# A hybrid encoder layer on one core: the merge of the next block's inverses is emitted directly behind a block's chain

## The chip, the core and the metric

The kernel runs on one of the eight cores of a Trainium2 chip. A core has TensorE (PE, matrix multiply; its weight loads are listed as PEld), VectorE (DVE), ScalarE (ACT), GpSimd (POOL) and SyncE (SP), which only issues transfers here. Each engine executes its own instructions in a fixed order and waits for others by semaphores. Transfers between memory and the core's buffers run on 16 DMA engines. TensorE writes to a small accumulator memory (PSUM), from which VectorE or ScalarE take the results.

The metric is the time of one execution in device microseconds; less is better.

## The reference

One layer of an encoder in float32 for 1024 positions of width 1024: a half-step gated feed-forward, a mixer with two groups of eight heads, and a second half-step feed-forward, each with norms around it. One group is dilated attention, the other a forward and a backward scan of the generalized delta rule. The scan is where the change lies:

```python
def _rwkv7_step(state, inp):
    r, w, k, v, kk, kka = inp
    sa = jnp.einsum('dbhvk,dbhk->dbhv', state, kk)
    state = state * w[..., None, :] - sa[..., :, None] * kka[..., None, :] + v[..., :, None] * k[..., None, :]
    y = jnp.einsum('dbhvk,dbhk->dbhv', state, r)
    return state, y
...
x = x + post1(FFN1(pre1(x))) * 0.5
x = x + post2(concat(attn, rwkv) @ w_out)
x = x + post3(FFN2(pre3(x))) * 0.5
```

(The last three lines are the layer in short form.) A state is 64 by 64 for each head and direction.

## The kernel before

**Stages.** The first feed-forward, the input projection and the attention come first, then the scan (from about 1250 to 1560 us of the span), then the finish of the scan's heads, the output projection, and the second feed-forward. Only the scan's order is touched.

**Chunks and blocks.** The scan goes by chunks of 64 positions, two chunks to a block: 16 chunks, 8 blocks (`NB`), both directions and all eight heads at once. Within a chunk the recurrence is solved as a triangular system, for which an inverse of a 64 by 64 unit triangular matrix is needed for each chunk, direction and head: 32 of them a block. Each block passes four steps:

- `prep(n)` (L789) loads the block's inputs, forms the decayed factors on VectorE and ScalarE, multiplies them on TensorE into `lp` (L836), masks the products on VectorE into `lm` (L838), transposes keys into `bt` (L844, L846), and stores the diagonal 32 by 32 parts of `lm` to memory (`x_d`, L852, on SyncE's queue).
- `solve(n)` (L856) loads these parts spread over partitions (`X`, L861), inverts the 32 by 32 triangles in 31 steps of two VectorE instructions each (L872, L874) and transposes the result back into `X` (L876).
- `merge(n)` (L879) makes the 64 by 64 inverses of the 32 by 32 ones. Per block: 128 small matmuls into the accumulator `pa` (L889), a ScalarE copy of it into `tt` (L890); 64 matmuls with the off-diagonal part of `lm` (L894), two copies into `tt` (L896) and one into `am` (L897); 64 matmuls (L900) and two copies with the sign changed into `tt` (L902). Each group of matmuls waits for the copy ahead of it.
- `chain(n)` (L918) runs the recurrence for the block's two chunks. ScalarE first overwrites a part of `lm` with `pr` (L928), which has to wait until the merge has read `lm`. Then for each chunk: `xu` from the state `sv` (L941), a copy `xs` (L944), the product of the inverses `tt` with `xs` (L952), a signed copy into `uv` (L954), the new state `st` and the output `y` (L937 at the helper's line), the state scaled on VectorE (L968), and `y` copied into `yb` (L970) and stored.

**Buffers.** Block data (`lm`, `pr`, `bt`, `gc`) has three places, `R0`, `R1` and `B0`, taken in turn, so `prep(n + 3)` can start writing only when `chain(n)` has let its place go. `X` has two buffers: `solve(n + 3)` takes over that of `solve(n + 1)`, which `merge(n + 1)` reads last. `tt` has two tiles, by the parity of the block. The accumulator `pa` has one buffer, so the first matmuls of a merge wait until the merge before has copied it out.

**Attended tiles.** `project_attended` (L1066) multiplies a tile of 128 rows of the attention's output by its half of the output weights: a load (`yat`), a scaling, four transposes (`yq`), a split into two parts, and twice twelve matmuls (`po`, shown at L1064). It does not depend on the scan and is spread over the loop: tiles 0 and 1 after chain 0, then 2, 3 and 4, then 5 and 6 after chain 4, and 7 after chain 5.

**What sets the order.** The program names the engine of each instruction, and its order of emission gives each a rank. When the program is built, a planner goes through the whole graph on a timeline of its own. For each engine it takes, among the instructions whose inputs and buffers are ready on that timeline, the one emitted earliest. So instructions of several steps lie mixed on an engine, and a step emitted earlier goes first where both could run. On the chip that order is fixed: an instruction whose input comes later than planned holds up everything behind it on its engine.

The loop (L1289 to L1306) first merges block 0, prepares and solves block 2 (0 and 1 came before), then goes over the blocks: merge of the block (from block 1), its chain, then `upto(n + 3)`, which prepares and solves block n + 3 if there is one, then the attended tiles. For n of 5 and more `upto` does nothing.

Of the kernel before, what the change touches and what calls it, by code (L numbers as in the profile page):

```python
# [163 lines left out]
class _Kernel:  # L164
# [1002 lines left out]
    def run(self):  # L1167
# [5 lines left out]
        with self.top as top:  # L1173
# [86 lines left out]
            NB, s_sr, s_pr, s_zr, s_pm = NC_ // BLK, ExitStack(), ExitStack(), ExitStack(), ExitStack()  # L1260
# [5 lines left out]
            pm = self.pool(s_pm, "ps_m", 1, space=PSUM, **R)  # L1266
# [4 lines left out]
            blk = {}  # L1271
# [7 lines left out]
            sc = self.pool(s_sc, "scan")  # L1279
# [9 lines left out]
            def upto(m):  # L1289
                while nxt[0] <= min(m, NB - 1):  # L1290
                    n = nxt[0]
                    blk[n] = self.prep(n, sp, pp, (R0, R1, B0)[n % 3])
                    blk[n]["inv"] = self.solve(n, sp)
                    nxt[0] += 1
# [3 lines left out]
            upto(2)  # L1298
            WA = self.out_weights(eo, 0, self.aog)
            for n in range(NB):  # L1300
                if n:
                    self.merge(n, blk[n], sc, pm)
                self.chain(n, blk.pop(n), sc, pc)
                upto(n + 3)
                for t in {0: [0, 1], 1: [2], 2: [3], 3: [4], 4: [5, 6], 5: [7]}.get(n, []):
                    self.project_attended(eo, sc, pe, t, WA, rs_a)  # L1306
# [133 lines left out]
```

## Time and profile before

| | |
|---|---|
| median of 3 runs | 2345.42 us (2341.84 to 2350.2) |
| profiled execution | 2343.05 us, of which the span from first to last instruction is 2341.3 us |
| mean granted TensorE clock | 0.969 |
| 62 instructions of one solve (L872, L874), each | about 0.25 us |
| a chain, from L941 of its first chunk to its last scaled state | about 14 to 20 us |
| a block, from chain to chain, blocks 1 to 5 | 36 to 45 us |

How to read the profile: times are microseconds, durations in group listings are nanoseconds. "L889" is line 889 of the kernel. `out<-in` names the tiles written and read. In a timeline, a row is start, duration, engine, line, operation, tiles, shape and count; the bracket at the end is the time that the engine stood idle just before, and what ended it. "issue" is time in which the engine waited for nothing that the profile names. In a table of waits a row is: engine and what waited, what it waited for, the sum in us, how often, the longest. The granted clock (PEclk) is TensorE's, as a share of full speed. Ends of matmuls are modelled, since they overlap.

### The profile page before, as it was taken

What the parts mean: (1) busy time and instruction counts of PE and PEld (TensorE: products, weight loads), DVE (VectorE), ACT (ScalarE), POOL (GpSimd) and SP (SyncE); (2) the same over time, 40 slices, a digit from 0 to 9 for tenths busy, and PEclk for the clock granted to TensorE, in tenths of its full rate; (3) what the DMA queues carried; (4) which work ended last, traced back from release to release, by engine and by line L of the source; (5) the groups of instructions that cost most, each with busy time, mean ns of one, the idle gap of its engine ahead of it and who ended that gap; (6) DMA issues with size and microseconds to landing.
All of it is one profiled execution on the core that took longest, in us unless ns stands there. A gap on an engine that the chain in (4) does not pass through costs nothing. (4 is left out here: it accounts for less than half of the span.)

```text
span 2341.3 us, 41376 instructions
## 1 busy us (share of the span) xinstructions
PE 2206.1 (94%) x15556; PEld 1783.6 (76%) x15556; DVE 1768.5 (76%) x2870; ACT 1031.8 (44%) x1958; POOL 551.5 (24%) x662
## 2 busy tenths in 40 slices
PE   6999999999999998999996998988799999999997
PEld 4788888878877676788775777765578888887886
DVE  8899999965676244666668877737899999996565
ACT  4323232354577412666555555454442323235443
POOL 6244444410000010111111111122424444441000
PEclk8999999999999999999997999989899999999999
DMA  5244545486672514443268655467435454548665
GB/s 154 97 165 167 171 148 172 153 269 191 195 229 83 219 46 123 119 115 99 62 174 222 174 155 161 113 205 267 154 113 170 168 171 147 173 154 269 193 191 178
DMA packets 357148, 381.97 MB, mean 163 GB/s; under 512 B 73042, under 2 KB 264402, under 8 KB 356948
## 3 DMA queue, kind: packets, MB, share of 16 engines
q1 hardware_dynamic: 309088, 278.53, 39.5%
q0 software_dynamic: 27504, 88.14, 9.9%
q10 hardware_dynamic: 20356, 12.66, 1.8%
q8 instruction: 122, 2.00, 0.4%
q14 instruction: 78, 0.64, 0.1%
HBM read 256.49 MB, written 122.75 MB: 162 GB/s over the span
## 5 line engine op out<-in xcount | busy, mean ns | idle before, releaser
L186 ACT ACTIVATE wh<-raw 128x512 fp32r<-128x512 f32 (+1 forms) x273 | 168.2, 627 | 271.2 <-DVE raw L62 93.6
L187 DVE TENSOR_TENSOR wl<-raw,wh 128x512 fp32r<-128x512 f32 (+1 forms) x273 | 278.7, 1023 | 6.0 <-ACT wh L186 5.2
L81 PE MATMUL gu<-xh,wh 128*128 128x512 f32 x704 | 278.3, 396 | 1.2 <-ACT xh L186 0.8
L81 PE MATMUL gu<-xl,wh 128*128 128x512 f32 x704 | 276.6, 393 | 0.0
L81 PE MATMUL gu<-xh,wl 128*128 128x512 f32 x704 | 276.2, 392 | 0.0
L415 PE MATMUL pd<-gl,gwh 128*128 128x512 f32 x616 | 240.3, 390 | 2.3 <-DVE gl L187 2.3
L415 PE MATMUL pd<-gh,gwh 128*128 128x512 f32 x616 | 239.5, 390 | 0.6 <-DVE row L86 0.6
L415 PE MATMUL pd<-gh,gwl 128*128 128x512 f32 x616 | 239.7, 389 | 0.0
L86 DVE TENSOR_TENSOR row<-gu,row 128x512 f32<-128x512 f32 x308 | 206.3, 681 | 23.9 <-PE gu L81 23.1
L187 DVE TENSOR_TENSOR gwl<-graw,gwh 128x512 fp32r<-128x512 f32 (+1 forms) x176 | 117.9, 672 | 127.7 <-ACT gwh L186 126.9
L116 POOL DMA_DIRECT2D d_hid<-row x154 | 84.7, 551 | 473.1 <-DVE row L114 447.6
L186 ACT ACTIVATE gwh<-graw 128x512 fp32r<-128x512 f32 (+1 forms) x176 | 101.4, 576 | 186.3 <-PE pd L415 154.3
L81 PEld LDWEIGHTS gu<-xh,wh 128*128 128x128 f32 x704 | 133.9, 190 | 30.1 <-ACT xh L186 2.0
L81 PEld LDWEIGHTS gu<-xl,wh 128*128 128x128 f32 x704 | 133.9, 190 | 27.7
L81 PEld LDWEIGHTS gu<-xh,wl 128*128 128x128 f32 x704 | 133.5, 190 | 27.9
L415 PEld LDWEIGHTS pd<-gl,gwh 128*128 128x128 f32 x616 | 115.6, 188 | 27.4 <-DVE gl L187 3.7
L415 PEld LDWEIGHTS pd<-gh,gwh 128*128 128x128 f32 x616 | 115.5, 188 | 25.3 <-DVE row L86 1.0
L415 PEld LDWEIGHTS pd<-gh,gwl 128*128 128x128 f32 x616 | 115.7, 188 | 24.0
L187 DVE TENSOR_TENSOR gl<-raw,gh 128x512 fp32r<-128x512 f32 x160 | 113.6, 722 | 18.1 <-ACT gh L186 17.7
L94 ACT ACTIVATE row<-row 128x512 f32<-128x512 f32 x44 | 27.9, 633 | 221.6 <-DVE row L86 214.1
L145 POOL TENSOR_TENSOR ws<-ws 128x512 f32<-128x512 f32 x88 | 114.3, 1299 | 1.2
L186 ACT ACTIVATE gh<-raw 128x512 fp32r<-128x512 f32 x160 | 98.0, 621 | 35.3 <-DMA raw<-in_ffn_w_down_dram 25.5
(354 smaller groups left out, 5254.3 us busy)
## 6 DMA issues: line engine op xcount, KB each, us to landing
d_hid<-row POOLq DMA_DIRECT2D x154, 256.0 KB, 2.4
graw<-d_hid SPq DMA_DIRECT2D x132, 256.0 KB, 3.2
raw<-in_ffn_w_gate_dram SPq DMA_DIRECT2D x88, 256.0 KB, 3.1
raw<-in_ffn_w_up_dram SPq DMA_DIRECT2D x88, 256.0 KB, 3.4
ws<-in_ffn_w_down_dram SPq DMA_DIRECT2D x88, 256.0 KB, 4.6
d_ws<-ws POOLq DMA_DIRECT2D x88, 256.0 KB, 2.3
raw<-d_ws SPq DMA_DIRECT2D x88, 256.0 KB, 2.9
raw<-in_ffn_w_down_dram SPq DMA_DIRECT2D x66, 256.0 KB, 3.5
```

The lines of the kernel that those rows point to most:

```text
L81: self.K.nc.tensor.matmul(ps, a[:, k, :], b[:, k, :], start=(k == 0 and i == 0), stop=(k == 3 and i == 2))
L86: add = lambda o, x: V.tensor_tensor(o, ps, x, op=OP.add)
L94: A.activation(y[:, 0], y[:, 0], AF.Silu)
L116: put = lambda n, y: G.dma_start(self.hid[n - 1, j // 2], y)
L145: G.tensor_tensor(o, a, b, op=OP.subtract)
L186: self.nc.scalar.activation(h, src, AF.Copy)
L187: (eng or self.nc.vector).tensor_tensor(l, src, h, op=OP.subtract)
L415: T.matmul(ps[x], a[:, ts], b, start=(m == 0 and k == 0), stop=(m == NM - 1 and k == 2))
```

## The change

The merge of block n + 1 is emitted directly behind the chain of block n, ahead of the preparation and the solve of block n + 3 and of the attended tiles. Before, it was emitted behind these, directly ahead of its own chain. Merge 0 stays in front of the loop. No instruction, buffer or argument differs.

```diff
             for n in range(NB):
-                if n:
-                    self.merge(n, blk[n], sc, pm)
                 self.chain(n, blk.pop(n), sc, pc)
+                if n + 1 < NB:
+                    self.merge(n + 1, blk[n + 1], sc, pm)
                 upto(n + 3)
                 for t in {0: [0, 1], 1: [2], 2: [3], 3: [4], 4: [5, 6], 5: [7]}.get(n, []):
                     self.project_attended(eo, sc, pe, t, WA, rs_a)
```

## The prediction

> **What bounds the kernel now.** I read the busy table first, then the busy time block by block, then the waits of TensorE, then the timelines. A change of order can only win back time in which the bounding engine stands still in the part that it touches.
>
> ```profile
> span 2341.3 us, 41376 instructions
> ...
> PE 2206.1 (94%) x15556; PEld 1783.6 (76%) x15556; DVE 1768.5 (76%) x2870; ACT 1031.8 (44%) x1958; POOL 551.5 (24%) x662
> ```
>
> TensorE is busy for 94% of the span, and the diff touches the scan alone. I cut the scan at the ends of the blocks' chains (the second scaled state, L968) and asked for the busy time of each stretch: chain 1 to chain 5, then chain 6, then chain 7.
>
> ```profile
> core 0: us, PE busy (x) PEld busy (x) DVE busy (x) ACT busy (x) POOL busy (x), PEclk, DMA share, GB/s
> 1304.60:1350.00 45.40, 41.94 (x797) 34.36 (x795) 39.82 (x121) 23.89 (x46) 5.82 (x12) 0.96 0.58 166
> 1350.00:1389.80 39.80, 35.70 (x775) 30.37 (x773) 29.16 (x82) 21.18 (x41) 5.43 (x12) 0.87 0.58 160
> 1389.80:1426.30 36.50, 33.19 (x667) 28.08 (x665) 28.39 (x78) 21.34 (x42) 6.68 (x13) 1.00 0.63 176
> 1426.30:1469.40 43.10, 36.47 (x720) 30.63 (x720) 34.95 (x106) 21.34 (x41) 5.49 (x10) 0.88 0.49 136
> 1469.40:1511.90 42.50, 41.04 (x739) 33.30 (x736) 33.39 (x102) 19.82 (x37) 4.90 (x9) 1.00 0.40 113
> 1511.90:1537.20 25.30, 23.80 (x687) 19.72 (x685) 10.46 (x33) 11.55 (x22) 4.40 (x8) 1.00 0.30 86
> 1537.20:1562.60 25.40, 21.88 (x481) 17.86 (x481) 6.75 (x13) 14.51 (x26) 9.72 (x9) 0.87 0.95 297
> ```
>
> TensorE bounds every stretch. Its idle time (stretch less busy) is 3.46, 4.10, 3.31, 6.63, 1.46, 1.50 and 3.52 us: 24.0 us in all, or 1.0% of the run, and the first five hold 19.0 of it. VectorE is next, with 28.4 to 39.8 us a block. No order can gain much more than these idle times and what the slowed clock adds to them (0.87 and 0.88 in two of the five).
>
> The waits of TensorE between 1300 and 1550 us say what the idle time is:
>
> ```profile
> PE lp L836 <- DVE lm L838: 7.8, 9, 2.2
> PE pa L889 <- issue: 3.7, 2, 1.8
> PE xu L952 <- ACT xs L944: 2.6, 2, 1.6
> PE pa L889 <- ACT tt L902: 2.0, 2, 1.4
> PE pa L900 <- issue: 1.7, 1, 1.7
> PE pa L900 <- ACT am L897: 1.6, 2, 1.3
> ...
> PE pa L894 <- ACT tt L890: 0.9, 1, 0.9
> ```
>
> 9.9 of these 20.3 us stand ahead of matmuls of the merge (L889, L894, L900). So the merge is worth placing well, though its own work is small.
>
> **The change part by part.** It adds and removes no instruction. Merges 1 to 6 move; 0 does not. Merges 1 to 5 pass one preparation with its solve and one or two attended tiles, merge 6 passes attended tile 7 alone. Merge 7 stays where it was, because after chain 6 nothing is left to prepare or to project. A merge issues 256 matmuls and six ScalarE copies, and no DMA: it goes past no transfer on SyncE's, GpSimd's or ScalarE's queue.
>
> ```profile
> 1334.69 0.85 PE L889 MATMUL pa<-ident,X 32*32 32x32 f32 x44 [1.85 <-issue]
> ...
> 1361.35 1.07 PE L894 MATMUL pa<-X,lm 32*32 32x32 f32 x56 [0.94 <-ACT tt L890]
> ...
> 1369.48 1.20 PE L900 MATMUL pa<-tt,am 32*32 32x32 f32 x64 [0.23 <-ACT am L897]
> ...
> 1372.73 0.64 PE L889 MATMUL pa<-ident,X 32*32 32x32 f32 x30 [1.42 <-ACT tt L902]
> 1373.35 1.97 PE L952 MATMUL xu<-xs,tt 64*64 64x64 f32 x32
> ...
> 1384.66 1.10 PE L952 MATMUL xu<-xs,tt 64*64 64x64 f32 x32
> ...
> 1411.73 1.15 PE L952 MATMUL xu<-xs,tt 64*64 64x64 f32 x32 [1.58 <-ACT xs L944]
> ```
>
> On ScalarE, the last two copies of merge 3 and the copy behind them in its queue:
>
> ```profile
> 1409.90 1.17 ACT L902 ACTIVATE tt<-pa 32x512 f32<-32x512 f32 x2
> 1411.09 0.58 ACT L944 COPY xs<-xu 128x512 f32<-128x512 f32 x1
> ```
>
> By these rows 64 matmuls take about 1.2 us, a merge therefore at most 4.8 us of TensorE and, at six copies of 0.58, 3.5 us of ScalarE. This work is the same at either place, so moving it counts zero; only waits count. The rows of TensorE are merge 2: it begins at 1334.69, and its last copy (L902) ends only just before 1372.73, the very moment at which chain 2 needs it (L952). Its input, the transposed inverse of solve 2, was there all that time:
>
> ```profile
> 1333.55 1.04 DVE L876 STREAM_TRANSPOSE X<-Ti 128x512 f32<-128x512 f32 x1
> ```
>
> From 1334.6 to 1372.7 the merge was spread between attended and preparation matmuls, 38 us for some 8 us of work. With the change it ranks directly behind chain 1, so it should end some 10 us after chain 1, and chain 2 has its inverse and may overwrite the masks that L894 reads (L928) while the preparation still runs.
>
> The terms, in the time of the profiled execution:
>
> 1. Waits of the next merge for the one `pa` buffer (L889 behind L902): 2.0 us, gone, because the merge before has long ended. Ends 0 and 2.0.
> 2. Waits inside moved merges, 0.94 + 0.23 (merge 2; 3, 4 and 5 show none): 1.2 gained. The rest of the L900 rows, 1.33 and 1.74, belongs to merge 7 and stays.
> 3. Chains that wait for `xs` because ScalarE had L902 in front of it: 2.6 gained. Ends 0 and 2.6.
> 4. Preparation matmuls that wait for VectorE's mask product: 7.8. With its inverse early, the next chain has matmuls ready to fill such gaps, as two of its kinds already do. The order is fixed when the program is built, so only gaps that the planner foresees are filled. Ends 0 and 7.8; I take a third, 2.6.
> 5. The clock. After the wait of 1.42 us the row of L952 is 1.97 us against 1.10 for the same 32 matmuls later in the block. The stretch from 1374 to 1382 ran at half clock, all of it busy:
>
> ```profile
> 1374.00:1378.00 4.00, 4.00 (x107) 3.23 (x103) 2.49 (x4) 2.11 (x5) 0.00 (x0) 0.50 0.87 249
> 1378.00:1382.00 4.00, 4.00 (x64) 3.85 (x64) 1.78 (x4) 0.26 (x1) 0.00 (x0) 0.50 0.43 123
> ```
>
> At most 4.0 of those 8 us come back if that wait does not happen; another wait may take its place, so I take 1.8. Ends 0 and 4.0.
>
> [...]
>
> 6. Waits that the move makes. The merge is a ladder of three matmul groups with ScalarE copies between them, and it now stands in front of the work that used to lie between its rungs. Preparation and attended tiles can still be pulled into the gaps. Lower end 0. The upper end is merge 7, which already stands directly behind a chain, with nothing behind it:
>
> ```profile
> 1540.71 0.33 PE L941 MATMUL xu<-sv,lm 128*64 128x64 f32 x2 [0.20 <-ACT lm L928]
> 1542.38 1.43 PE L900 MATMUL pa<-tt,am 32*32 32x32 f32 x57 [1.33 <-ACT am L897]
> 1545.55 0.42 PE L900 MATMUL pa<-tt,am 32*32 32x32 f32 x7 [1.74 <-issue]
> ```
>
> That is 3.27 us of waits; five merges would lose 16.4. With cover, merges 2 to 5 lost 1.2 together, 0.3 each. I take 0.4 each, 2.0, nearer to the covered ones, since attended tiles remain behind each of the five.
>
> 7. Counted at nothing: the preparation starts its matmuls up to 4.8 us later, and VectorE's mask products with them. What covers it is the solve of the block before, which keeps VectorE busy then and is not needed until a block later; without that cover it would be up to 4.8 us a block. The two waits of L889 for a solve (3.7) stay: its first matmuls already stand inside the chain, and xu's L952 and all after it wait behind them. Buffer `X`, which solve n+3 takes over from merge n+1, comes free sooner, but its load waits for the mask blocks written to memory just before. Merge 6 passes one attended tile in a stretch with 1.50 us idle: 0.
>
> Sum: 2.0 + 1.2 + 2.6 + 2.6 + 1.8 - 2.0 = 8.2 us gained. The profiled execution took 2343.05 us, its span and 1.75 us around it; it would take 2334.9. The median shown, 2345.42, lies 2.4 above it, so the forecast for the median is 2337.2. What lies behind the scan moves along by the same amount, since it starts from the last chains.
>
> **The rivals.**
>
> A larger gain: chain n+1 runs all through the preparation and hides it. All idle of the five blocks goes but the two solve waits, 19.0 - 3.7, and the clock's 4.0: about 19 us, 2326. For it speaks that the solve is a block ahead; against it that VectorE has up to 39.8 of 45.4 us in a block and TensorE 41.04 of 42.50.
>
> No change: the matmuls only change places in a full queue, terms 4 and 5 come to nothing and term 6 eats terms 1 to 3. 5.8 gained against five times 1.2: 2345. For it speaks that in the block from 1469.4 merge 5 costs hardly any idle time where it is.
>
> Slower: the ladder of the merge is uncovered, as in merge 7. Its place is the end of each chain, where the preparation's first VectorE steps have only just been released and the attended tile waits for its load or its transposes, so TensorE has nothing to put between L889, L894 and L900. Price: 16.4 less the 5.8 of terms 1 to 3, 10.6 us: 2356. It decides from 2.0 us of uncovered wait in each merge, where it equals gains 1 to 5 (10.2 us over five). Against it: merges 2 to 5 found enough to put between, and the same attended tiles are still there.
>
> That the planner leaves the order as it was cannot be: it goes by the order of emission wherever two instructions are ready, and the 38 us of merge 2 show how far down its place in the program put it.
>
> **How the numbers follow.** The forecast has 0.45, the larger gain 0.08, no change 0.20, slower 0.27. A measurement of this kernel can tell about 0.3%, 7.0 us, from no change. The forecast's own range is 2331 to 2343, so 0.62 of it, 0.28, lies past that bound (below 2338.4). Faster is 0.28, the larger gain's 0.08 and 0.01 of no change: 0.37. Same is the forecast's other 0.17 and 0.18 of no change: 0.35. Slower is its case's 0.27 and the last 0.01 of no change: 0.28. The range runs from just past the larger gain, 2325, to just past the slower case, 2357.
>
> **What would show it.** Right: L902 of merge n+1 ends within about 12 us of chain n's last state; the waits of L889 for L902 are gone; the stretches between ends of chains 1 to 4 shrink by 1 to 3 us each; the clock from chain 1 to chain 2 is above 0.87. Wrong: idle of over 2 us a block ahead of L894 and L900, or ahead of the preparation's L836, or VectorE idle between chain and preparation. If the stretches shrink but the end does not come earlier, the loss lies in the tail after chain 6, which I took as unchanged.

## The result, and the profile after

Over 20 runs each, the changed kernel took 2346.39 us and the kernel before 2345.56: ratio 1.0001, 95% interval 0.9988 to 1.0014. No gain or loss can be told. Single executions of the changed kernel took 2333.51 to 2352.33 us, so what follows, read from one execution of each kernel, shows where time went and not the median to a microsecond. The profiled execution took 2341.57 us, with a span of 2339.8. The page of the changed kernel, its busy table and its transfer queues:

```profile
span 2339.8 us, 41361 instructions
...
PE 2197.5 (94%) x15556; PEld 1776.8 (76%) x15556; DVE 1766.2 (75%) x2870; ACT 1031.1 (44%) x1958; POOL 552.9 (24%) x662
...
q8 instruction: 122, 2.00, 0.4%
```

The last line, of a part of the page that I had not used, turns out to matter: the queue that brings instructions moved 122 packets, 2.00 MB.

The scan cut again at the ends of the chains, from chain 0 to chain 7 (start and end, then the length, then the busy times):

```profile
core 0: us, PE busy (x) PEld busy (x) DVE busy (x) ACT busy (x) POOL busy (x), PEclk, DMA share, GB/s
1305.80:1351.30 45.50, 40.17 (x762) 33.45 (x763) 36.85 (x112) 23.75 (x44) 5.95 (x13) 0.92 0.62 163
1351.30:1392.40 41.10, 36.40 (x731) 30.29 (x732) 30.90 (x90) 21.46 (x41) 5.13 (x11) 0.92 0.56 155
1392.40:1434.10 41.70, 34.05 (x784) 28.92 (x783) 31.44 (x92) 23.16 (x45) 5.64 (x12) 1.00 0.58 154
1434.10:1470.50 36.40, 34.32 (x664) 28.67 (x664) 31.88 (x92) 20.28 (x40) 6.12 (x13) 0.91 0.61 170
1470.50:1513.70 43.20, 40.47 (x738) 33.07 (x734) 30.70 (x94) 19.22 (x36) 5.16 (x9) 0.92 0.37 111
1513.70:1539.00 25.30, 24.29 (x617) 20.08 (x616) 13.70 (x42) 12.08 (x23) 3.76 (x7) 1.00 0.28 84
```

The blocks took 45.5, 41.1, 41.7, 36.4, 43.2 and 25.3 us, against 45.4, 39.8, 36.5, 43.1, 42.5 and 25.3 before: one longer by 5, one shorter by 7, and together 233.2 against 232.6. TensorE's waits between 1300 and 1550 us:

```profile
PE pa L900 <- issue: 6.4, 4, 2.4
PE pa L889 <- issue: 5.0, 3, 2.2
PE lp L836 <- DVE lm L838: 2.9, 5, 0.9
PE xu L941 <- ACT lm L928: 2.5, 2, 2.3
PE y L937 <- issue: 1.8, 1, 1.8
PE pa L900 <- ACT am L897: 1.3, 1, 1.3
PE lp L836 <- issue: 1.2, 1, 1.2
...
PE pa L889 <- DVE X L876: 0.2, 1, 0.2
...
PE pa L894 <- ACT tt L890: 0.2, 1, 0.2
```

The waits for a named engine that the change was meant for have shrunk: L836 for the masks from 7.8 to 2.9 us, L889 for L902 (2.0) and L952 for `xs` (2.6) have no row left. In their place stands "issue": nine waits of 14.4 us in all (6.4 + 5.0 + 1.8 + 1.2), where before there were three of 5.4, and two of those three, 3.7 us, ended together with a solve.

Where the new waits stand, in TensorE's timeline:

```profile
1350.07 0.99 PE L889 MATMUL pa<-ident,X 32*32 32x32 f32 x93
1352.04 0.27 PE L889 MATMUL pa<-ident,X 32*32 32x32 f32 x9 [0.99 <-issue]
...
1356.17 0.62 PE L900 MATMUL pa<-tt,am 32*32 32x32 f32 x27
1358.26 0.76 PE L900 MATMUL pa<-tt,am 32*32 32x32 f32 x37 [1.46 <-issue]
```

These two stand in the middle of a group. The 93 matmuls of L889 ahead of the first wait and the 9 behind it read the same finished `X`, write the same `pa` and wait for nothing new. So no other engine is seen to hold them. I counted every record of TensorE's two sequences (matmuls, weight loads and the waits of the queue) up to the end of each stall, and set beside it the packet of the instruction queue that had begun last, on the same clock:

```
stall ends   idle ahead   instructions before it   remainder by 256   packet, start to end
1307.23      1.94         15297                    193                1303.38 to 1305.74
1313.16      1.51         15553                    193                1310.75 to 1311.66
1352.04      1.18         16833                    193                1349.16 to 1350.58
1358.26      1.65         17089                    193                1355.93 to 1356.88
1383.32      2.41         17857                    193                1380.95 to 1381.89
1399.44      1.52         18625                    193                1397.18 to 1398.17
1425.80      1.99         19393                    193                1423.53 to 1424.41
1476.58      1.40         21441                    193                1474.05 to 1474.93
1547.77      2.60         24257                    193                1545.25 to 1546.43
```

(Idle here goes from start to start, so it is some 0.2 us more than in the timeline.) All nine stand at the same remainder, and each ends 1.3 to 1.7 us behind the end of a packet. Each of the 122 packets is 16,384 bytes; the 31,112 matmuls and loads over 122 packets make 255 each. So TensorE gets its instructions in pieces of 256, as the nine equal remainders show, and in the new order it runs out of them. One f32 matmul of the merge is two matmuls and two loads in the trace (the 64 of L889 are 128 and 128), so a merge is 512 instructions, exactly two pieces, and small matmuls in a row use up a piece in some 2.4 us (128 at 1.2 us for 64), those of L889 faster (93 in 0.99 us above). The moved merges are not run without a break: from the first matmul of L889 to the last of L900 merges 1 to 6 took 14 to 22 us, against 20 to 38 before, and at most 204 of a merge's instructions follow each other without others between, against 150. Closer than before, though: the 256 instructions ahead of each of the first eight stalls went in 2.0 to 5.3 us. In the kernel before, one stall in the scan has this remainder: the 1.74 us ahead of merge 7's last seven matmuls. The two waits of L889 stand at 196 and 243 there.

With this, the scan from the end of chain 0 to that of chain 6 can be added up for both kernels. The two rows, before and after:

```profile
1304.59:1537.23 232.64, 212.15 (x4366) 176.47 (x4362) 176.20 (x518) 119.16 (x228) 32.73 (x60) 0.95 0.51 142
```

```profile
1305.77:1539.04 233.27, 209.70 (x4283) 174.48 (x4283) 175.51 (x519) 119.98 (x227) 31.79 (x60) 0.94 0.52 143
```

| us, chain 0 to chain 6 | before | after | difference |
|---|---|---|---|
| TensorE busy, as at full clock (busy less half of the time at half clock) | 200.2 | 196.0 | -4.2 |
| lost to the half clock (half of 23.9 and 27.3 us) | 11.95 | 13.65 | +1.7 |
| stalls at remainder 193 (by the timeline's idle time) | 0 | 12.0 (8) | +12.0 |
| other idle time of TensorE | 20.5 | 11.6 | -8.9 |
| sum | 232.6 | 233.3 | +0.6 |

The move did win back some nine microseconds of waits, and stalls for instructions took their place. A part of the 4.2 us is only that 83 fewer matmuls lie in this stretch (4366 and 4283), since merge 1 now begins before the end of chain 0. On the chain of work that ended last stand five of these eight stalls, 7.7 us, and in the kernel before, of "issue" waits of this size, only the two behind a solve, 3.7 us. The longest of the five:

```profile
1381.10 2.22 issue
```

### The profile page after: what moved, and what is told of

Its sections match the earlier page's. It is cut to its first block, busy times and chain, and to the rows that moved or that the text cites. A ratio compares the mean times of both kernels' runs of the same rounds, so it can differ in the third digit from the quotient of the medians.

```text
span 2339.8 us, 41361 instructions
## 1 busy us (share of the span) xinstructions
PE 2197.5 (94%) x15556; PEld 1776.8 (76%) x15556; DVE 1766.2 (75%) x2870; ACT 1031.1 (44%) x1958; POOL 552.9 (24%) x662
## 4 chain that ended last, share of the span: by engine, by line
PE 37%; DVE 6%; DMA 5%; issue 3%; ACT 2%; POOL 0%; SPq 0%; DVEq 0%; POOLq 0%; ACTq 0%
PE gu L81 16%; PE pd L415 9%; DMA in<-d_rk 2%; PE zr L510 2%; PE po L1064 1%; PE st L937 1%; PE lp L836 1%; DMA wor<-in_w_out_dram 1%; PE po L705 1%; DVE Ti L874 1%; DVE ttmp L872 1%; PE pw L1064 1%; PE xu L941 1%; PE y L937 1%; PE pt L698 1%
## 5 line engine op out<-in xcount | busy, mean ns | idle before, releaser
L81 PEld LDWEIGHTS gu<-xl,wh 128*128 128x128 f32 x704 | 133.2, 189 | 27.3
L415 PEld LDWEIGHTS pd<-gh,gwh 128*128 128x128 f32 x616 | 115.6, 188 | 25.3 <-DVE row L86 1.0
L415 PEld LDWEIGHTS pd<-gh,gwl 128*128 128x128 f32 x616 | 115.6, 188 | 23.9
```

Source lines behind the costliest of these rows:

```text
L81: self.K.nc.tensor.matmul(ps, a[:, k, :], b[:, k, :], start=(k == 0 and i == 0), stop=(k == 3 and i == 2))
L415: T.matmul(ps[x], a[:, ts], b, start=(m == 0 and k == 0), stop=(m == NM - 1 and k == 2))
```

## The experiments

Two theories. S, supply: the gains are real and are given back because a closely packed merge outruns the delivery of TensorE's instructions. The rival in the first four runs was F: the moved matmuls only change places in a full queue, and the issue waits are an accident of the data or of one execution. After these, the rival was V: VectorE's lateness with the masks holds the scan, whatever TensorE waits for.

**Fewer instructions.** One matmul in place of the 64 small ones of L889 (its result is not theirs: the transposes are left out), in both orders:

```diff
-        for j in range(NI):
-            for r in [r for lo, hi in lohi for r in (hi, lo)]:
-                T.matmul(pa[r, j, :], D[r, j, :], self.ident[r, r], start=True, stop=True)
+        T.matmul(pa.rearrange("p j c -> p (j c)"), self.ident, D.rearrange("p j c -> p (j c)"), start=True, stop=True)
```

> The order of before, with the 64 small transposing matmuls of L889 (128 records, 2.08 us of TensorE a merge) replaced by one matmul of 128x512 that writes the same accumulator (2 records, about 2.1 us); the transposes are left out. Theory S (supply): TensorE's instructions arrive in pieces of 256, weight loads counted, at best one piece in 3.4 us, and small matmuls in a row use one up in 2.4 us. In the order of before the merge's matmuls lie among bigger ones and only one such stall (1.7 us) stands in the scan, so little changes: ratio to before 0.997 to 1.001, at most 3 us of issue waits in the scan. Theory F (full queue): the moved matmuls only change places between busy engines: 1.000 as well.

> The same replacement in the changed order: again 2 records for 128 with about the same TensorE time, the transposes left out. Theory S: a merge has 260 instructions in place of 512, one piece and not two, so the nine issue waits of the changed kernel (14.4 us in the scan) fall to at most four (under 6 us) and the gains of the new order appear: 6 to 12 us below the kernel before, ratio 0.995 to 0.9975, and below fat_before by about as much. Theory F: nothing is gained, 1.000 to before and to fat_before.

Measured: 2336.13 us in the order of before (ratio 0.9969, 0.9955 to 0.9983) and 2333.76 in the changed one (0.9961, 0.9947 to 0.9976). No stall of the changed order is left. Its waits between 1300 and 1550 us, without the finish of the heads (`yc`):

```profile
PE lp L836 <- DVE lm L838: 6.7, 5, 2.4
...
PE bp L844 <- DVE lm L838: 2.4, 2, 1.4
PE pa L887 <- DVE X L876: 2.0, 2, 1.3
PE po L1062 <- DVE yal L1076: 1.7, 2, 1.3
```

There is no row "issue" of note any more, and against the changed kernel the scan from chain 0 to chain 6 fell by 5.9 us, from 233.3 to 227.4. The changed order's time lies in the range of S, and F, which had 1.000 for both, missed twice. But S missed the order of before by a little (0.9969 under its 0.997), and it had promised the new order about 6 to 12 us over the old one with the same matmul; it has 2.4, which these intervals do not tell from nothing. Of the 12.0 us of stalls 7.5 came back as other idle time (11.6 to 19.1 us), most of it waits for VectorE. The order of before also gained 4.7 us in the scan, without having had a stall there to lose. So the two times do not show what the stalls cost. The one matmul also took work from TensorE: it took 1.1 us and not the 2.1 expected, here in the changed order, where the 128 records of L889 add some 1.6 (12.5 ns each, as worked out further below).

```profile
1460.37 1.12 PE L887 MATMUL pa<-X,ident 128*128 128x512 f32 x2
```

One reservation goes for all kernels here but the next: any change of an instruction lets the planner put others elsewhere.

**The same order, half a piece later.** In the changed kernel, 32 matmuls of merge 0 are executed twice; of the remaining order only a handful of rows differ.

```diff
-        for j in range(NI):
+        for j in (list(range(NI // 2)) if n == 0 else []) + list(range(NI)):
```

> The changed kernel with 32 of L889's matmuls executed twice in merge 0 (64 records, 128 instructions, half a piece; the order of the rest stays). Theory S: the issue waits stand where the count of TensorE's instructions, weight loads included, passes 193 beyond a multiple of 256, as all nine of the changed kernel do; so they move by 128 instructions against the work: at most two of the nine at the same matmul as before, and all over 1 us at that count. Theory F, or any cause that lies in the data: they stay at the same matmuls (after 26 of L889's in merge 3, after 35 in merge 1, after two of y in chain 2).

Two of its largest stalls in the timeline:

```profile
1304.14 1.07 PE L894 MATMUL pa<-X,lm 32*32 32x32 f32 x56 [2.67 <-issue]
...
1351.26 0.75 PE L894 MATMUL pa<-X,lm 32*32 32x32 f32 x20 [3.57 <-issue]
```

None of its stalls is at a matmul of the list above, and all stand at remainder 193 of the new count: the stalls moved against the work, by the count alone. That is S. The scan was no shorter for having a smaller sum of them (11.0 us from start to start between the ends of chain 0 and chain 6, against 13.6): 238.3 us, with 41 us at half clock. Its one execution took 2341.78 us in all.

**The supply by itself.** In the order of before, L889 of merge 0 is executed five times, 640 records in a row (`list(range(NI)) * (5 if n == 0 else 1)`).

> The order of before, with L889's matmuls of merge 0 executed five times in a row (640 records, 1280 instructions, five pieces; every other merge as it was). Theory S: after the first piece or two, 128 records take 3.4 to 4.0 us each and at least two gaps of 1 us or more stand at the count 193 beyond a multiple of 256; the run takes 14 to 18 us. Theory F: small matmuls keep their pace of 64 in 1.2 us, without gaps: 12 us.

```profile
1255.87 2.07 PE L889 MATMUL pa<-ident,X 32*32 32x32 f32 x156
1257.87 0.66 PE L611 MATMUL vt<-ident,vrev 128*128 128x128 f32 x4
1258.45 0.87 PE L889 MATMUL pa<-ident,X 32*32 32x32 f32 x78
1261.39 1.28 PE L889 MATMUL pa<-ident,X 32*32 32x32 f32 x128 [2.06 <-issue]
1267.32 1.93 PE L889 MATMUL pa<-ident,X 32*32 32x32 f32 x128 [4.66 <-issue]
1275.17 1.93 PE L889 MATMUL pa<-ident,X 32*32 32x32 f32 x128 [5.92 <-issue]
1278.90 0.54 PE L889 MATMUL pa<-ident,X 32*32 32x32 f32 x22 [1.80 <-issue]
```

This is the plainest view of it. The first 234 matmuls run without a stall; from there on they come in portions of 128, one piece each, and TensorE stands still before each. The run took 23.6 us, more than the 14 to 18 of S. The pieces began 5.6, 8.1 and 3.6 us apart, and the row of the transfers' share suggests a reason:

```profile
core 0: us, PE busy (x) PEld busy (x) DVE busy (x) ACT busy (x) POOL busy (x), PEclk, DMA share, GB/s
1259.00:1264.60 5.60, 1.60 (x166) 1.37 (x153) 5.05 (x19) 1.75 (x3) 3.54 (x6) 0.96 0.81 197
1264.60:1272.70 8.10, 1.93 (x128) 1.79 (x128) 2.90 (x9) 0.72 (x1) 1.25 (x3) 0.50 1.09 275
1272.70:1276.30 3.60, 1.13 (x85) 1.13 (x88) 0.00 (x0) 0.00 (x0) 0.00 (x0) 0.50 0.13 39
```

One piece came 3.6 us after the other with the transfer engines nearly idle (share 0.13), and one 8.1 us after the other with them full (1.09). That the traffic slows the pieces is read from these three rows; it was not tested alone. The packets themselves took 1.06, 1.08 and 1.12 us, so a delay by traffic would lie ahead of a packet's start.

**VectorE early.** The solve with 8 of its 31 steps (`range(8)` for `range(31)` in L871), in both orders, without and with the single matmul for L889.

> The order of before, with 8 of the solve's 31 steps (46 of its 62 VectorE instructions left out, some 11 us of VectorE a block). Theory S (supply of instructions): VectorE is not what holds the scan, but the waits of lp for the mask products go: 5 to 8 us less than before, ratio 0.9965 to 0.998, and at most one stall at the count 193. Theory V (VectorE's lateness holds TensorE in either order): 10 us less or more, ratio 0.9957 or below.

> The same shortened solve in the changed order. Theory S: the stalls at the count 193 stay (six or more of them, 8 us or more between 1250 and 1560 us), so it is no faster than the shortened solve in the order of before: ratio to the kernel before 0.997 to 1.000. Theory V: with VectorE early the moved merge is free, 10 us less or more, 0.9957 or below, and below the shortened order of before by 3 us or more.

> Shortened solve and one matmul of 128x512 for L889's small ones, in the order of before. Theory S: as the kernel with the one matmul (0.9969) less the waits for mask products: 0.994 to 0.996. Theory V: 10 us below the kernel with the one matmul, 0.9925 or less.

> Both in the changed order. Theory S: no stall at the count 193 of 1 us or more, and 8 to 14 us below the changed order with the shortened solve alone: 0.992 to 0.995. Theory V: the one matmul makes no difference once VectorE is early: within 3 us of the changed order with the shortened solve alone.

| median us, ratio to before (95%) | order of before | changed order |
|---|---|---|
| 8 steps | 2346.11, 1.0014 (1.0000 to 1.0029) | 2336.74, 0.9973 (0.9959 to 0.9986) |
| 8 steps, one matmul for L889 | 2333.78, 0.9963 (0.9947 to 0.9978) | 2316.40, 0.9897 (0.9877 to 0.9918) |

V falls for the order of before: 62 us of VectorE in the scan gone (176.2 to 114.6 us busy from chain 0 to chain 6) and no gain. S missed it as well: it had 5 to 8 us less and the waits for the masks gone. These grew, from 7.8 to 14.5 us between 1300 and 1550 us:

```profile
PE bp L844 <- DVE lm L838: 11.2, 5, 3.3
PE lp L836 <- DVE lm L838: 3.3, 2, 2.8
```

So less work on VectorE did not bring the masks earlier, and this is no clean test of V. In the changed order with 8 steps S had no gain over the old one, with six or more stalls; there were five, 8.1 us in all from start to start, only two of them (4.1 us) between the ends of chain 0 and chain 6, and it was 9 us faster than the old order. V had at least 3 us of that, but at most 0.9957 to the kernel before, and missed there. With the one matmul too, the old order lies just outside the range of S (0.9963 over 0.996) and far from V's 0.9925; the changed order is 20.3 us below the changed order with 8 steps alone, where S had 8 to 14 and V at most 3.

With both edits the changed order is worth 17.4 us (2333.78 to 2316.40), more than S gave it; in the profiled executions, 8.2 us of that lies between the ends of chain 0 and chain 6. In the changed order the two edits together (0.9897) bring more than each alone (0.9961 and 0.9973) added up, by little more than the intervals allow for. That fits two limits of which each hides a part of what lifting the other would bring. One would be the supply; that the other is VectorE is not shown, since waits for the masks remain with both edits (8.5 us, L836 and L844).

**A merge with half the instructions.** VectorE transposes straight into `tt`, in both orders:

```diff
-        for j in range(NI):
-            for r in [r for lo, hi in lohi for r in (hi, lo)]:
-                T.matmul(pa[r, j, :], D[r, j, :], self.ident[r, r], start=True, stop=True)
-        A.copy(tt[:, :, 32:64], pa)
+        self.nc.vector.transpose(tt[:, :, 32:64], D)
...
         for lo, hi in lohi:
-            A.copy(tt[lo, :, 0:32], pa[lo])
-        A.copy(am, pa)
+            A.copy(tt[lo, :, 0:32], tt[lo, :, 32:64])
+        for lo, hi in lohi:
+            A.copy(am[hi], pa[hi])
```

> The order of before, with the transposes of the merge done by VectorE straight into tt (one instruction, about 1.04 us as the solve's own transpose) in place of the 128 records of L889 and the first ScalarE copy. TensorE loses 2.1 us a merge, VectorE gets 1.04. Theory S: 256 of a merge's 512 instructions are gone, no stall of 1 us or more at the count 193 in the scan, and TensorE's saving counts: 8 to 16 us less, ratio 0.993 to 0.9965. Theory V: VectorE, which the masks wait for, is later by 1 us a block, and most is given back: 0.997 or above.

> The same in the changed order. Theory S: no stall of 1 us or more, and the new order is worth 4 to 10 us to the kernel with VectorE's transposes in the old one: 0.990 to 0.995. Theory V: the waits for mask products take the place of the stalls, as with the one matmul (6.7 and 2.4 us there): within 3 us of VectorE's transposes in the order of before.

Measured: 2324.76 us in the order of before (0.9921, 0.9897 to 0.9944) and 2319.51 in the changed one (0.9888, 0.9864 to 0.9912). Both beat both kernels, by more than S had it. The transposes cost VectorE 0.71 us each in the listing, not 1.04. The changed order of these, its instruction queue and its first waits of TensorE between 1300 and 1550 us:

```profile
q8 instruction: 114, 1.87, 0.3%
```

```profile
PE lp L836 <- DVE lm L838: 9.6, 5, 2.6
PE yc L993 <- POOL f_y L992: 5.1, 1, 5.1
PE xu L939 <- DVE sv L966: 2.4, 4, 1.3
```

Eight pieces fewer, no "issue" wait in place of nine, and what is left are mostly waits for the masks (9.6 us). By the medians the move is worth 5.3 us here, in the range of S (4 to 10) and above V's 3, but the two intervals overlap and the profiled executions do not bear it out: from chain 0 to chain 6 the changed order took 222.4 us and the order of before 220.7, the former with 41.0 us at half clock against 23.9. So a gain by the move is not shown here; the gain of both kernels over the kernel before is.

**Other places for the merge.** Only L889 and its copy directly behind the chain, the rest ahead of its own chain (`merge` gets a last argument: 1 for the first part, 2 for the rest); and the whole merge behind the preparation and the solve, ahead of the attended tiles:

```diff
+                if n:
+                    self.merge(n, blk[n], sc, pm, 2)
                 self.chain(n, blk.pop(n), sc, pc)
                 if n + 1 < NB:
-                    self.merge(n + 1, blk[n + 1], sc, pm)
+                    self.merge(n + 1, blk[n + 1], sc, pm, 1)
```

> Only the first part of the merge of block n + 1 (L889 and its copy) directly behind chain n; the rest (L894 to L902) where it was before, directly ahead of chain n + 1. Nothing is left out. Theory S: at most 256 instructions in a row, one piece: at most four stalls of 1 us or more between 1250 and 1560 us, under 7 us in all (nine, 16.2 us, in the changed kernel), and the waits of L889 for tt are gone: ratio 0.9965 to 0.9995. Theory V: within 0.1% of before.

```diff
+                upto(n + 3)
                 if n + 1 < NB:
                     self.merge(n + 1, blk[n + 1], sc, pm)
-                upto(n + 3)
```

> The merge of block n + 1 behind the preparation and the solve of block n + 3, but ahead of the attended tiles. Nothing is left out. Theory S: its matmuls lie between those of the preparation, so at most five stalls of 1 us or more, under 8 us: 0.9965 to 0.9995. Theory V: within 0.1% of before.

Both miss. The split took 2356.10 us (1.0043, 1.0023 to 1.0064), the middle place 2348.37 (1.0020, 1.0004 to 1.0036). The split has few stalls, as S says (4.3 us), but its waits are

```profile
PE lp L836 <- DVE lm L838: 16.1, 4, 8.5
PE pa L891 <- issue: 4.3, 4, 2.4
```

with a single one of 8.5 us for the masks, and 64.9 us at half clock from chain 0 to chain 6. Half of that is lost, 32.4 us, 20.5 more than before, and the stretch is 20.7 us longer. The middle place has five stalls of 1 us or more and a sixth, 12.4 us from start to start where S allowed 8, and every issue wait of 0.9 us or more in it stands at remainder 193. Few stalls are not enough for a gain: this is where S alone fails, and why the split has so much half clock and so long a wait was not followed further.

## Why the prediction was right and wrong

The time lies in the range and within what I could tell from no change, but the range of 2325 to 2357 us held four different cases, so that it holds the time says little. The likeliest case, 8.2 us faster, did not happen. By its steps:

- **Term 1, `pa`:** right; the 2.0 us are gone.
- **Term 2, waits inside the merges (1.2):** right; 0.2 of L894 is left, and the 1.3 of L900 is merge 7's, as before.
- **Term 3, `xs` behind L902 (2.6):** right; no such row.
- **Term 4, masks:** the mechanism was right, a third was too little: 7.8 became 2.9, so 4.9 and not 2.6, of which 0.8 came back ahead of L844.
- **Term 5, the clock (1.8 gained):** wrong in sign. From chain 1 to chain 2 the clock rose from 0.87 to 0.92 as I wanted, but over six blocks the time at half clock went from 23.9 to 27.3 us.
- **Term 6, new waits (2.0, at most 16.4): the step that failed.** I looked for waits of the ladder, matmul against copy, and of these only 0.2 us came in the moved merges; the cover I had named, preparation and attended tiles, did its work. What came was 12.0 us of stalls for instructions from chain 0 to chain 6, 9.0 of it inside the moved merges. The price was in the rows that I had quoted: of merge 7's 3.27 us, the 1.74 "issue" is such a stall, and I had counted it as a rung of the ladder. The seven matmuls behind it read the same finished tiles as the 57 ahead of it, so no dependency was left to wait for; I should have asked what else it is, and what becomes of it in six merges packed alike. Beside them, L941 now waits 2.5 us for L928 (0.2 before) and 1.2 for `sv`, and the attended tiles (L1064) 2.2 us for their split parts (0.3 before), which no term held.
- **Term 7:** the solve waits of 3.7 did not stay. The merge still starts just behind its solve (the transposed inverses of solves 1, 3, 4 and 5 end 0.05 to 0.7 us before the first matmul of L889), but TensorE now has other work until then, and L889 waits for `X` 0.2 us. That the same work at either place counts zero is not refuted. The busy time of L889 between 1300 and 1545 us did fall, before and after:

```profile
L889 PE MATMUL pa<-ident,X 32*32 32x32 f32 x896 | 14.7, 204 | 5.6 <-issue 3.7 <-ACT tt L902 2.0
```

```profile
L889 PE MATMUL pa<-ident,X 32*32 32x32 f32 x896 | 12.5, 194 | 5.2 <-issue 5.0 <-DVE X L876 0.2
```

But before, a part of them ran at half clock, which cost 1.9 us, and after none. Where overlapping matmuls are counted once and as at full clock, one of L889 adds 12.4 ns before and 12.5 after.

Of the signs named beforehand, the waits of L889 for L902 are gone, the clock from chain 1 to chain 2 is above 0.87 (0.92), and the first held: L902 of merges 1 to 6 ended 6 to 12 us behind the chain (merge 2, for instance, 8.9 us behind chain 1):

```profile
1359.06 1.19 ACT L902 ACTIVATE tt<-pa 32x512 f32<-32x512 f32 x2 [0.92 <-PE pa L900]
```

Of the stretches between the ends of chains 1 to 4 two grew and one shrank (39.8, 36.5 and 43.1 us to 41.1, 41.7 and 36.4). The rival "no change" gave the right time, and in two points the right reason, that the new waits eat terms 1 to 3 and that the clock gives nothing; that the gain ahead of the masks comes to nothing was wrong. The slower rival's uncovered ladder did not appear.

What stays open: what the changed order would take with its own exact sequence and no stalls. No kernel here could hold the order and cut the instructions. With the single matmul the scan of the changed order is 5.9 us shorter, but so is that of the order of before, by 4.7, so how much of the 12.0 us would be had is not known; the table with the shortened solve suggests that a second limit takes a part.

## What to carry to other kernels

When an order of small matmuls is tightened, count instructions as well as microseconds: here TensorE used up the 256 instructions ahead of a stall in as little as 2.0 us, and the closest two deliveries of the changed kernel began 3.39 us apart. Its nine "issue" waits, 14.4 us in all, stood at one remainder of the instruction count, and moved with the count when half a piece was put in: they were waits for instructions. What helped here was fewer instructions (VectorE's one transpose for 128 matmuls and loads, 0.9921 without the move and 0.9888 with it); two other places of the merge also had a smaller sum of stalls, and were 0.2 and 0.4% slower than the kernel before. And a gain that vanishes may have been taken by two limits: lift both before the idea is given up.

## What the runs showed of the hardware that I had not expected

- TensorE gets its instructions in packets of 16,384 bytes, 256 instructions (122 packets for 31,112 matmuls and loads, in both kernels). In the changed kernel the closest two packets began 3.39 us apart, in the kernel before 3.56, those of the 640 matmuls in a row 3.6 to 8.1 us. A stall that began just as a packet set out (1380.91, packet from 1380.95) lasted 2.4 us.
- From chain 0 to chain 6 of the changed kernel 26 of the 34 boundaries between pieces cost at most 0.2 us, but 8 stopped TensorE for 1.0 to 2.2 us each; in the kernel before none of its 34 there did.
- Between the ends of chain 0 and chain 6 TensorE's clock was at half speed in stretches of 3.4, 10.2, 6.8 and 3.4 us in the kernel before, and of 6.8, 3.4, 3.4, 6.8 and 6.8 us in the changed one. In the changed kernel four of the five begin within 2.6 us of the end of a stall (at 1313.0, 1360.8, 1384.7 and 1476.9), so a stall may cost more than itself. That was not tested, and the changed order with the one matmul, which has no stall, has the same 27.3 us at half clock. Nor does the length of a wait alone decide: one of 1.46 us (to 1358.26) was followed by a stretch, one of 2.29 us (to 1405.66) was not. So term 5's reading, that the wait of 1.42 us brought the stretch at half clock behind it, is not shown.
